# Two of four channel blocks of a depthwise convolution as diagonal fp32 matmuls, in a one-core decoder layer

## The chip, the cores and the metric

One Trainium2 chip, one of its cores, one launch. The metric is the device time of one execution in microseconds (us). Changes of under 0.5% are not told from no change here. Engines are named as the profile names them: PE (TensorE's matmuls), PEld (its weight loads), DVE (VectorE), ACT (ScalarE), POOL (GpSimd) and SP (SyncE, which issues most DMAs).

## The reference, cut to what matters

One layer: a wide input projection, sliding window attention beside a gated causal convolution, an output projection with a layer norm, a product-key mixture of 16384 experts (PEER), and a gated embedding with a second layer norm. The change touches the convolution alone, which has 512 channels and 31 taps per channel:

```python
def conv_group(a, gate, conv_w, conv_b, ln_g, ln_b):
    h = a * jax.nn.sigmoid(gate)
    h = lax.conv_general_dilated(
        h, conv_w[:, None, :].astype(h.dtype), window_strides=(1,),
        padding=((CONV_WIDTH_K - 1, 0),),
        dimension_numbers=('NWC', 'WIO', 'NWC'),
        feature_group_count=CONV_WIDTH) + conv_b
    h = layer_norm(h, ln_g, ln_b)
    return jax.nn.silu(h)
...
        attn = sliding_window_attention(q, k, v, sinks[i])
        conv = conv_group(ca, cg, conv_w[i], conv_b[i], conv_ln_g[i], conv_ln_b[i])
        mixed = jnp.concatenate([attn, conv], axis=-1) @ w_out[i]
        x = layer_norm(DEEPNORM_ALPHA * x + mixed, ln1_g[i], ln1_b[i])
        r = DEEPNORM_ALPHA * x + peer(x, peer_query[i], peer_keys[i], peer_u[i], peer_v[i])
```

The sizes are 1024 tokens and a model width of 1024, in float32.

## The kernel before, in words

The 1024 tokens are 8 tiles of 128. Group A is the first 3 tiles (384 tokens), whose experts are gathered row by row; group B is the other 5 (640 tokens, "dense"), whose experts are computed as full matrix products. Exact products are made of three fp32r matmuls each: an operand is split into a high and a low part (ACT casts the high part `wh` or `acth`, DVE subtracts for the low part `wl` or `actl`), and `mm3` multiplies high by high, high by low and low by high. Attention scores, the values and the sums of the convolution's layer norm are plain fp32 matmuls.

The front of the kernel is made of streams, generators that each yield after a piece of work: `s_x` transposes x, `s_conv` makes the gated input `hc` of the convolution for one block of 128 channels (channels on partitions, 30 tokens of halo and then the group's tokens), `s_taps` applies the 31 taps, `s_qkv` and `s_att` are the attention, `s_cln` is the convolution's layer norm, `s_wout` the output projection and `s_ln1` the first layer norm. Suffix 0 or 1 of a stream is group A or B. The table `ORDER` interleaves the streams by hand in program order. From that program order the framework's scheduler, at build time, fixes the order in which each engine works through its own instructions, and at run time every engine takes them strictly in that order. So an instruction that waits holds up all that stands behind it on its engine.

Before, `s_taps(1)` does for each of four blocks one `tensor_scalar` (line 353, with the bias) and 30 `scalar_tensor_tensor` (line 355) on DVE, each over 128 channels by 640 tokens, accumulating into `cv`. It yields four times a block, 16 times in all, and `ORDER` spreads these 16 steps among the attention of group A and B (`a0`, `a1`), the taps of A and `w0`, the output projection of A. Attention takes a tile of tokens and one of two head groups at a time: PE scores into two PSUM tiles `pt` (line 394), DVE scales and masks them (398) and finds the maxima (404), ACT takes the exponentials (410) and divides (415), PE transposes the probabilities (426), ACT copies them (427), PE multiplies them with the values (430). The PSUM ring `pt` has two buffers, so the scores of one head group and the transposes of another take turns on it.

After the front come the query and top-k stage of A, and then two long stages (`s_early` with the u table and `s_dense` with the v table), in which PE multiplies nearly without a pause while the gathered rows of A run on POOL and DVE.

Of the kernel before, what the change touches and what calls it, by code (L numbers as in the profile page):

```python
# [8 lines left out]
F32 = mybir.dt.float32  # L9
# [4 lines left out]
AF = mybir.ActivationFunctionType  # L14
OP = mybir.AluOpType
# [4 lines left out]
P = 128  # L20
# [6 lines left out]
TAPS = 31  # L27
# [11 lines left out]
SB = 16  # L39
UB = 7  # L40
ROWLAG = 3
LAG = 2
AHEAD = 3
SPILL = 80
# [25 lines left out]
def n_split(n):  # L70
    k = -(-n // 512)
    while n % k or (n // k) % 2:
        k += 1
    return [(i * (n // k), n // k) for i in range(k)]
# [22 lines left out]
def layer(tc, io):  # L97
    nc = tc.nc
# [43 lines left out]
    def ph():  # L142
        return PP.tile([P, 512], F32, name="ph", bufs=4)
# [18 lines left out]
    ident = C.tile([P, P], F32, name="ident")  # L162
# [20 lines left out]
    def page(shape, dt, name):  # L183
        return PG.tile(shape, dt, name=name, tag="page", bufs=PAGES)
# [32 lines left out]
    chan = W_.tile([P, 3, 4], F32, name="chan")  # L217
    cw = W_.tile([P, 4, TAPS], F32, name="cw")
# [126 lines left out]
    def s_taps(gi):  # L345

        n = len(groups[gi]) * P
        cv[gi] = W_.tile([P, 4, n], F32, name="cv", tag=f"cv{gi}")
        for bl in range(4):
            hc, o = cin[gi, bl], cv[gi][:, bl, :]  # L350
            for t in range(TAPS):
                if t == 0:
                    nc.vector.tensor_scalar(o, hc[:, :n], cw[:, bl, 0:1], chan[:, 0, bl:bl + 1], op0=OP.mult, op1=OP.add)
                else:
                    nc.vector.scalar_tensor_tensor(o, hc[:, t:t + n], cw[:, bl, t:t + 1], o, op0=OP.mult, op1=OP.add)
                if t % 8 == 6:
                    yield

    def s_att(gi):

        later = []
        for j, i in enumerate(groups[gi]):
# [73 lines left out]
            for g in range(2):  # L436
                later.append((values, g, scores(g)))
                if len(later) > LAG:
                    f, *a = later.pop(0)
# [318 lines left out]
    def s_gather():  # L758

        for i in GA:  # L760
# [6 lines left out]
            def fetch(table, s):  # L767
                t = G.tile([P, D], F32, name="row", bufs=UB)
                nc.gpsimd.indirect_dma_start(out=t, out_offset=None, in_=table,  # L769
                                             in_offset=bass.IndirectOffsetOnAxis(ap=ids[i][:, s:s + 1], axis=0))  # L770
                return t
# [24 lines left out]
            for f, table, n in order:  # L796
                late.append((f, *divmod(n, SB), fetch(table, n)))
                if len(late) > ROWLAG:
                    g, *a = late.pop(0)
# [19 lines left out]
    def const():  # L819
        constants()  # L820
        yield

    streams = dict(x0=s_x(0), x1=s_x(1), k=const(), c0=s_conv(0), c1=s_conv(1), t0=s_taps(0), t1=s_taps(1), q0=s_qkv(0), q1=s_qkv(1),
                   a0=s_att(0), a1=s_att(1), l0=chain(s_attput(0), s_cln(0)), l1=chain(s_attput(1), s_cln(1)),
                   w0=s_wout(0), w1=s_wout(1), n0=s_ln1(0), n1=s_ln1(1), y=s_query(0), h=s_choose(0), u=early, g=s_swap(), r=rows)
# [90 lines left out]
    n = len(outs) * -(-P // SET)  # L916
# [106 lines left out]
```

## Time and profile before

| | |
|---|---|
| median of 3 runs | 2925.62 us (2921.28 to 2936.11) |
| the profiled execution's own time | 2930.05 us |
| its span in the profile | 2928.2 us |
| mean granted TensorE clock | 0.975 of full speed |
| busy: PE, DVE, ACT, POOL | 95%, 83%, 41%, 37% of the span |
| taps of group B on DVE | 116.5 to about 312 us of the span |

The profile is one execution. A busy time is the time in which at least one instruction of the engine was running, and a granted clock of 1.00 is 2.4 GHz, one of 0.50 is 1.2 GHz. A window's clock in between is a mean over stretches at either level. Idle time of an engine matters only where another one waits for it, so the views used are the windows around the convolution, the chain of work that ended last, and the timeline of single engines.

### The profile page before, as it was taken

To read this page: it belongs to the slowest core of one execution; us is meant where nothing else is said; L and a number is where in the kernel's file an instruction comes from. 1 tells how busy PE (TensorE), PEld (TensorE's weight loads), DVE (VectorE), ACT (ScalarE), POOL (GpSimd) and SP (SyncE) were. 2 spreads that over 40 slices of the span, in tenths; PEclk is the share of its full clock that TensorE was granted. 3 is DMA by queue.
4 is the path that set the end of the run, shared out by engine and by line. 5 is a ranking of instruction groups with operands and counts; after the bars stand their busy time and mean duration, and the time that the engine had idled before them with its cause. 6 is when DMAs were issued, how large, how long until landed. Compare 5 with 4: busy or idle time off the path is not lost.

```text
span 2928.2 us, 47594 instructions
## 1 busy us (share of the span) xinstructions
PE 2794.5 (95%) x17615; PEld 2513.3 (86%) x17615; DVE 2437.2 (83%) x5461; ACT 1193.6 (41%) x2464; POOL 1078.1 (37%) x851
## 2 busy tenths in 40 slices
PE   8996899999999999999999999799899999999888
PEld 8974589999999999999999999687788787777688
DVE  7999768979989799999856666898899888778866
ACT  4454634433334788888622222222222222222143
POOL 0103010267600333443435555555454445444320
PEclk9996899999999999999999999999999999999999
DMA  5211343599913699999999999999999999989631
GB/s 158 76 51 40 99 127 103 183 369 321 349 60 113 239 352 344 334 346 338 364 352 328 338 337 343 364 357 358 352 356 360 358 371 348 323 309 316 215 125 53
DMA packets 324569, 778.11 MB, mean 266 GB/s; under 512 B 29137, under 2 KB 144337, under 8 KB 321776
## 3 DMA queue, kind: packets, MB, share of 16 engines
q0 software_dynamic: 110592, 402.70, 38.0%
q1 hardware_dynamic: 213744, 372.37, 36.5%
q8 instruction: 138, 2.26, 0.3%
q14 instruction: 95, 0.78, 0.1%
HBM read 683.75 MB, written 91.23 MB: 265 GB/s over the span
## 4 chain that ended last, share of the span: by engine, by line
PE 79%; DVE 11%; DMA 5%; issue 3%; ACT 2%; SPq 0%; POOL 0%; DVEq 0%; ACTq 0%; POOLq 0%
PE ph L158 15%; PE ph L159 14%; PE ph L160 14%; PE sum L159 6%; PE sum L158 5%; PE sum L160 5%; PE pv L750 4%; PE pt L659 3%; PE part L158 2%; PE part L159 2%; PE part L160 2%; DMA ge<-e_dr 2%; DVE ag L785 2%; DVE row L777 1%; DVE vl L150 1%
## 5 line engine op out<-in xcount | busy, mean ns | idle before, releaser
L769 POOL DMA_INDIRECT row<-in_peer_u_dram,ids x384 | 511.5, 1332 | 707.9 <-DVE ag L785 418.7
L769 POOL DMA_INDIRECT row<-in_peer_v_dram,ids x384 | 499.5, 1301 | 647.0 <-DVE row L777 480.0
L158 PE MATMUL ph<-acth,uu 128*128 128x320 f32 x2048 | 657.4, 321 | 0.1
L159 PE MATMUL ph<-actl,uu 128*128 128x320 f32 x2048 | 641.6, 313 | 0.0
L160 PE MATMUL ph<-acth,uu 128*128 128x320 f32 x2048 | 639.9, 313 | 0.0
L785 DVE SCALAR_TENSOR_TENSOR ag<-row,hb,ag 128x1024 f32<-128x1024 f32 x384 | 492.4, 1282 | 2.2 <-DMA row<-in_peer_v_dram,ids 1.3
L777 DVE SCALAR_TENSOR_TENSOR row<-row,x 128x1024 f32<-128x1024 f32 x384 | 467.9, 1222 | 5.5 <-DMA row<-in_peer_u_dram,ids 5.2
L158 PEld LDWEIGHTS ph<-acth,uu 128*128 128x128 f32 x2048 | 386.6, 189 | 1.4 <-ACT sg L558 0.4
L159 PEld LDWEIGHTS ph<-actl,uu 128*128 128x128 f32 x2048 | 386.9, 189 | 0.7
L160 PEld LDWEIGHTS ph<-acth,uu 128*128 128x128 f32 x2048 | 385.5, 189 | 0.4
L159 PE MATMUL sum<-vl,ah 128*128 128x512 f32 x896 | 353.7, 395 | 5.0 <-DVE vl L150 4.8
L158 PE MATMUL sum<-vh,ah 128*128 128x512 f32 x896 | 344.2, 397 | 4.2 <-ACT ah L154 2.8
L154 ACT CAST ah<-ge 128x640 fp32r<-128x640 f32 x128 | 93.3, 729 | 570.7 <-DVE ge L878 417.4
L160 PE MATMUL sum<-vh,al 128*128 128x512 f32 x896 | 267.4, 390 | 0.0
L661 ACT CAST uu<-pt 128x512 fp32r<-128x512 f32 x256 | 150.5, 590 | 190.8 <-PE pt L659 181.0
L745 ACT ACTIVATE o<-oo,rest 128x128 bf16<-128x128 bf16 x640 | 205.8, 399 | 21.4 <-DVE oo L740 16.6
L158 PEld LDWEIGHTS sum<-vh,ah 128*128 128x128 f32 x896 | 171.0, 191 | 45.4 <-ACT ah L154 5.4
L159 PEld LDWEIGHTS sum<-vl,ah 128*128 128x128 f32 x896 | 171.3, 191 | 43.2 <-DVE vl L150 7.1
L158 PE MATMUL part<-vh,ah 128*128 128x512 f32 x384 | 154.7, 403 | 47.2 <-ACT ah L154 30.1
L160 PEld LDWEIGHTS sum<-vh,al 128*128 128x128 f32 x896 | 168.5, 188 | 34.9
L150 DVE TENSOR_TENSOR vl<-raw,vh 128x1024 fp32r<-128x1024 f32 x128 | 154.7, 1220 | 40.8 <-ACT vh L154 40.4
L150 DVE TENSOR_TENSOR uu<-pt,uu 128x512 fp32r<-128x512 f32 x116 | 79.8, 689 | 127.7 <-ACT uu L661 118.9
(298 smaller groups left out, 5768.3 us busy)
## 6 DMA issues: line engine op xcount, KB each, us to landing
raw<-in_peer_v_dram SPq DMA_DIRECT2D x128, 512.0 KB
raw<-in_peer_u_dram SPq DMA_DIRECT2D x89, 512.0 KB
e_dr<-ge SPq DMA_DIRECT2D x128, 320.0 KB
g_dr<-stage SPq DMA_DIRECT2D x20, 2048.0 KB
ge<-e_dr SPq DMA_DIRECT2D x128, 320.0 KB
gt<-g_dr SPq DMA_DIRECT2D x21, 1920.0 KB
uraw<-in_peer_u_dram SPq DMA_DIRECT2D x39, 512.0 KB
wraw<-in_peer_query_dram SPq DMA_DIRECT2D x32, 512.0 KB
```

Source lines behind the costliest of these rows:

```text
L150: return eng.tensor_tensor(o, a, b, op=OP.subtract)
L154: nc.scalar.copy(hi, src)
L158: nc.tensor.matmul(ps, lh, rh, start=first, stop=False)
L159: nc.tensor.matmul(ps, lh, rl, start=False, stop=False)
L160: nc.tensor.matmul(ps, ll, rh, start=False, stop=last)
L659: nc.tensor.matmul(ps[:, k * P:(k + 1) * P], raws[c][:, (4 * h + k) * P:(4 * h + k + 1) * P], ident, is_transpose=True, start=k == 0, stop ...
L661: nc.scalar.copy(uu[:, 0], turned)
L745: nc.scalar.mul(o2[:, 2, e], oo[:, 1, e], rest[:, t + e:t + e + 1])
L750: nc.tensor.matmul(ps[:, e * P:(e + 1) * P], o2[:, m, e], oo[:, 0, e], start=m == 0, stop=m == 2)
L769: nc.gpsimd.indirect_dma_start(out=t, out_offset=None, in_=table, in_offset=bass.IndirectOffsetOnAxis(ap=ids[i][:, s:s + 1], axis=0))
L777: behind(nc.vector.scalar_tensor_tensor(u, u, 1.0, x1, op0=OP.mult, op1=OP.mult, accum_out=hb[:, e:e + 1]), marks, TIE)
L785: behind(nc.vector.scalar_tensor_tensor(ag, v, blocks[b][:, e:e + 1], ag, op0=OP.mult, op1=OP.add), marks, TIE)
```

## The change

For blocks 2 and 3 of group B the taps move from DVE to PE. For each tap a 128 by 128 matrix `diag` holds the tap's 128 channel weights on its diagonal, and the convolution is a sum over taps of `diag` times `hc` shifted by the tap, accumulated in two PSUM tiles `ph` of 320 tokens each. DVE builds the diagonal matrices, eight at a time, and ACT moves the sums out of PSUM and adds the bias. A block is now one step of the stream, and six empty steps at the end keep the count of `ORDER` at 16.

```diff
+PE_TAPS = [(1, 2), (1, 3)]
...
         for bl in range(4):
             hc, o = cin[gi, bl], cv[gi][:, bl, :]
+            if (gi, bl) in PE_TAPS:
+
+                pss = [ph()[:, :tn] for _, tn in n_split(n)]
+                for c0 in range(0, TAPS, 8):
+                    m = min(8, TAPS - c0)
+                    diag = page([P, 8, P], F32, "diag")
+                    nc.vector.tensor_tensor(diag[:, :m], ident[:, None, :].to_broadcast([P, m, P]),
+                                            cw[:, bl, c0:c0 + m, None].to_broadcast([P, m, P]), op=OP.mult)
+                    for t in range(c0, c0 + m):
+                        for ps, (t0, tn) in zip(pss, n_split(n)):
+                            nc.tensor.matmul(ps, diag[:, t - c0], hc[:, t + t0:t + t0 + tn], start=t == 0, stop=t == TAPS - 1)
+                for ps, (t0, tn) in zip(pss, n_split(n)):
+                    nc.scalar.activation(o[:, t0:t0 + tn], ps, AF.Identity, bias=chan[:, 0, bl:bl + 1])
+                yield
+                continue
             for t in range(TAPS):
...
+        for _ in range(3 * sum(g == gi for g, _ in PE_TAPS)):
+            yield
```

How the change moves instructions is seen in three places. First, PE before, where the scores of group B's first tile (`pt<-kT,qT`, line 394) stand: layer norm sums of A, then the scores, then the output projection of A (`ph<-wh,actah`).

```order
L430 MATMUL pv<-pT,vlast 64x256
L381 MATMUL pt<-ident,acc_99 128x128 x2
L469 MATMUL pv<-sq,ones 128x384 x3
L394 MATMUL pt<-kT,qT 128x128 x8
L158 MATMUL ph<-wh,actah 128x512
L159 MATMUL ph<-wl,actah 128x512
```

The same place on PE now (line numbers are 18 higher here, and 1 higher in `mm3`): behind the same scores stand all 62 tap matmuls of block 2 in one piece, and then the matmuls that make `hc` of block 3.

```order
L448 MATMUL pv<-pT,vlast 64x256
L399 MATMUL pt<-ident,acc_99 128x128 x2
L487 MATMUL pv<-sq,ones 128x384 x3
L412 MATMUL pt<-kT,qT 128x128 x8
L362 MATMUL ph<-hc,diag 128x320 x62
L159 MATMUL ph<-acth,wh 128x320
L160 MATMUL ph<-actl,wh 128x320
```

Those 48 `hc` matmuls of block 3 (`ph<-acth,wh` and its two partners) stood ahead of the scores before. Now they stand between the two pieces, and the output projection comes after the second piece:

```order
L159 MATMUL ph<-acth,wh 128x320
L160 MATMUL ph<-actl,wh 128x320
L161 MATMUL ph<-acth,wl 128x320
L362 MATMUL ph<-hc,diag 128x320 x62
L159 MATMUL ph<-wh,actah 128x512
L160 MATMUL ph<-wl,actah 128x512
L161 MATMUL ph<-wh,actal 128x512
```

So PE takes the 124 tap matmuls as two unbroken pieces, with nothing of the attention between them; the scores of the second head group come 12 matmuls of the output projection behind the second piece.

Second, DVE before, about 20 us after those first scores: between two operations of the attention (`sc`, `st`) there stand one or two taps (line 355) each time.

```order
L476 TENSOR_TENSOR cv<-cv,rstd 128x384 x4
L405 TENSOR_TENSOR st<-st,sink 128x4
L355 SCALAR_TENSOR_TENSOR cv<-hc,cw,cv 128x640
L404 TENSOR_REDUCE st<-sc 128x4
L355 SCALAR_TENSOR_TENSOR cv<-hc,cw,cv 128x640 x2
L406 TENSOR_TENSOR st<-sink,st 128x4
L355 SCALAR_TENSOR_TENSOR cv<-hc,cw,cv 128x640
```

The same place on DVE now: the diagonal matrices of block 3 are built, `hc` of block 3 is made, two low parts of weights follow, and then the second scores are taken up without a tap between.

```order
L494 TENSOR_TENSOR cv<-cv,rstd 128x384 x4
L358 TENSOR_TENSOR diag<-ident,cw 128x1024 x3
L358 TENSOR_TENSOR diag<-ident,cw 128x896
L340 TENSOR_TENSOR hc<-ph,sg 128x320
L151 TENSOR_TENSOR wl<-wraw,wh 128x1024
L340 TENSOR_TENSOR hc<-ph,sg 128x320
L151 TENSOR_TENSOR wl<-wraw,wh 128x1024
L416 SCALAR_TENSOR_TENSOR sc<-pt,mask 128x2x256 x2
L422 TENSOR_REDUCE st<-sc 128x4
```

The taps of blocks 2 and 3 have left DVE's queue, and the attention's operations stand next to one another.

## Rows read from the trace of the kernel before

**Rows 1.** The page, parts 1 and 4: busy us, share, instructions; the chain by engine.

```profile
PE 2794.5 (95%) x17615; PEld 2513.3 (86%) x17615; DVE 2437.2 (83%) x5461; ACT 1193.6 (41%) x2464; POOL 1078.1 (37%) x851
PE 79%; DVE 11%; DMA 5%; issue 3%; ACT 2%; SPq 0%; POOL 0%; DVEq 0%; ACTq 0%; POOLq 0%
```

**Rows 2.** Windows of the front: busy us by engine, granted clock (PEclk), DMA.

```profile
core 0: us, PE busy (x) PEld busy (x) DVE busy (x) ACT busy (x) POOL busy (x), PEclk, DMA share, GB/s
200.00:360.00 160.00, 123.81 (x579) 83.36 (x577) 134.51 (x220) 90.53 (x225) 23.50 (x28) 0.78 0.20 66
217.00:255.00 38.00, 23.77 (x116) 17.81 (x115) 38.00 (x51) 19.30 (x42) 19.72 (x22) 0.80 0.22 70
255.00:271.00 16.00, 15.21 (x54) 9.30 (x54) 12.85 (x20) 4.02 (x9) 3.78 (x6) 0.51 0.00 0
271.00:280.00 9.00, 1.94 (x18) 1.39 (x18) 8.25 (x15) 5.80 (x21) 0.00 (x0) 0.67 0.00 1
280.00:296.00 16.00, 14.58 (x55) 9.05 (x55) 15.21 (x27) 9.67 (x27) 0.00 (x0) 0.54 0.12 34
296.00:322.00 26.00, 24.71 (x130) 17.71 (x129) 21.48 (x40) 15.95 (x45) 0.00 (x0) 1.00 0.51 156
322.00:349.00 27.00, 16.74 (x82) 11.57 (x82) 18.86 (x38) 17.90 (x47) 0.00 (x0) 0.62 0.27 103
360.00:400.00 40.00, 39.76 (x224) 37.14 (x223) 31.71 (x113) 26.99 (x49) 6.57 (x8) 1.00 0.41 122
```

**Rows 3.** Instructions that write or read cv: ns shortest/median/longest, first and last start us.

```profile
L355 DVE SCALAR_TENSOR_TENSOR cv<-hc,cw,cv x240: 602/800/1631, 30.9 to 311.2; 128x384 f32<-128x384 f32 x60, 128x640 f32<-128x640 f32 x60
L462 PE MATMUL pv<-cv,ones x24: 432/433/590, 204.0 to 379.4; 128*128 128x320 f32 x16, 128*128 128x384 f32 x8
L353 DVE TENSOR_SCALAR cv<-hc,cw,chan x8: 468/542/610, 29.3 to 219.6; 128x384 f32<-128x384 f32 x4, 128x640 f32<-128x640 f32 x4
```

**Rows 4.** Groups by line and shape, 0 to 900 us: busy us, mean ns, idle before.

```profile
L355 DVE SCALAR_TENSOR_TENSOR cv<-hc,cw,cv 128x640 f32<-128x640 f32 x120 | 106.0, 910 | 0.0
L150 DVE TENSOR_TENSOR wl<-wraw,wh 128x1024 fp32r<-128x1024 f32 x76 | 94.2, 1240 | 50.7 <-ACT wh L154 25.5 <-PE pv L159 20.4 <-PE ph L159 2.1
L333 ACT ACTIVATE sg<-ph 128x320 f32<-128x320 f32 x8 | 3.5, 433 | 3.8 <-PE ph L160 3.8
L158 PEld LDWEIGHTS ph<-acth,wh 128*128 128x128 f32 x384 | 72.2, 188 | 1.0 <-ACT sg L333 0.4 <-issue 0.4
```

**Rows 5.** Timeline of PE: start us, us, instruction, count, idle before it and its releaser.

```profile
194.10 0.31 PE L159 MATMUL ph<-actl,wh 128*128 128x320 f32 x1
...
199.09 0.31 PE L160 MATMUL ph<-acth,wl 128*128 128x320 f32 x1
...
210.27 1.03 PE L426 MATMUL pt<-ident,sc 128*128 128x128 f32 x8
...
217.00 1.26 PE L394 MATMUL pt<-kT,qT 64*128 64x128 f32 x16
...
221.19 1.71 PE L394 MATMUL pt<-kT,qT 64*128 64x128 f32 x16
231.52 0.79 PE L158 MATMUL ph<-wh,actah 128*128 128x512 f32 x1 [8.62 <-ACT wh L154]
...
297.18 0.40 PE L158 MATMUL ph<-wh,actah 128*128 128x512 f32 x1
...
299.29 0.39 PE L158 MATMUL ph<-wh,actah 128*128 128x512 f32 x1
...
340.25 3.09 PE L394 MATMUL pt<-kT,qT 64*128 64x128 f32 x16 [1.02 <-DVE actal L150]
...
377.53 2.32 PE L462 MATMUL pv<-cv,ones 128*128 128x320 f32 x8
```

**Rows 6.** Timeline of ACT just before the first scores of group B.

```profile
211.23 0.59 ACT L427 COPY pT<-pt 128x512 f32<-128x512 f32 x1 [3.98 <-PE pt L426]
```

**Rows 7.** The chain of work that ended last, 254 to 297 us: start us, us, what.

```profile
255.38 1.13 PE pt L426 x4
...
258.29 1.04 PE pv L430 x2
259.33 2.00 PE pt L394 x8
261.33 1.90 PE pv L430 x6
...
273.61 0.80 DVE cv L355
...
275.01 0.79 DVE cv L355
...
276.54 1.59 DVE cv L355 x2
```

**Rows 8.** What PE waited for, 400 to 1700 us and 1700 to 2750 us, longest first.

```profile
PE pt L659 <- ACT uu L674: 3.4, 3, 1.6
...
PE part L158 <- ACT ah L154: 30.1, 8, 15.2
PE part L158 <- DVE acc L899: 11.9, 10, 2.0
```

## The prediction

> **What bounds the kernel now.** I read the page first. Over the whole span PE is busy 95% and DVE 83%, and PE holds 79% of the chain that ended last [rows 1]. By that alone, work moved from DVE to PE goes the wrong way; but the taps lie in one short stretch, and the stretch decides. So I read the windows next. From 200 to 360 us DVE is busy 134.51 of 160 us, PE 123.81, and the TensorE clock was granted at 0.78 on average [rows 2]. From 217 to 255 us DVE never stops (38.00 of 38.00), while PE is busy for 23.77 us. Here DVE is the limit, and the taps of blocks 2 and 3 are in its queue. From 360 us on PE is again busy 39.76 of 40 us at full clock [rows 2], and its longest wait up to 1700 us sums to 3.4 us [rows 8]. So what the front gains or loses is handed on whole. The chain says which of the taps are on the path between 255 and 296 us: 0.80, 0.79 and 1.59 us of them [rows 7]. The rest of the path there is PE at an average clock of 0.51 to 0.54 [rows 2].
>
> **What DVE is relieved of.** 60 `scalar_tensor_tensor` of 640 tokens leave, at 106.0/120 = 0.88 us each [rows 4], 53 us, and two `tensor_scalar` at about 0.6 us [rows 3]: 54 us. Eight builds of diagonal matrices come. The trace has none; the nearest row is the subtraction of 1024 fp32 elements at 1.24 us [rows 4], so about 9.5 us (one of four is shorter). If broadcast operands cost double, 20 us, and not under half of it, 5 us. Net, DVE loses some 44 us of 134.51.
>
> **What PE gets.** Plain fp32 matmuls of 320 columns are in the trace: 4 of them show as 8 records, which take 2.32 us with the last one's whole 0.432 us [rows 3, 5]. So records follow one another every (2.32 - 0.43)/7 = 0.27 us, and one matmul takes 0.54 us at full clock. A block is 31 taps by 2 halves: 62 x 0.54 = 33.4 us, both blocks 66.8 us. For comparison, an fp32r matmul of the same width follows the last every (199.09 - 194.10)/34 = 0.147 us [rows 5]. The one thing that could make a tap dearer is its own weight load; those last 0.188 us [rows 4], yet fp32r matmuls with new weights each come every 0.147 us, so loads are hidden there. I take 0.54 us; the upper bound, loads not hidden at all, adds 248 x 0.188 = 47 us. Below 0.54 us I see nothing, since the row has the same type and width.
>
> ACT gets four moves out of PSUM at 0.433 us [rows 4], 1.7 us. They wait for the pieces, and a cast of `wh` and the exponentials of the second scores are queued behind the second pair; but those exponentials wait for PE anyway, and the weights of the next 36 matmuls of the output projection are cast before.
>
> **Where it lands, step by step.** In the new order PE meets the first piece right behind the first scores of group B, which before started at 217.00 us [rows 5]. They come some 3 us sooner: ACT idled 3.98 us just ahead for transposes that stood behind output projection matmuls [rows 5, 6], and these now stand later. So the piece starts at 217 - 3 + 1.1 = 215 us (211 to 219). Its `diag` tiles are ready about then. It ends at 248.5. The 48 matmuls that make `hc` of block 3, moved here, take 48 x 0.147 = 7 us, to 255.6; DVE's copy adds about 0.6 us; the second piece ends at 289.6 us.
>
> DVE meanwhile waits at the diagonals of block 3 for page buffers that the first piece holds, and behind them stand `hc` of block 3 and two low parts of weights. The first three follow as taps finish, and PE has the 7 us of `hc` matmuls to do; so this is hidden, and at worst, all four built late, it costs some 5 us.
>
> Next PE has 84 matmuls of the output projection, at (299.29 - 297.18)/9 = 0.234 us [rows 5], 19.7 us, two more sets of scores at 1.2 us (16 records in 1.26) and six transposes at 0.13 us (8 in 1.03 [rows 5]): 22.9 us. It then reaches the first transposes of group B's probabilities at 312.5 us. Before, they stood at 255.38 us [rows 7]. The change is 57 us late there: two pieces and the moved matmuls (74 us) against about 17 us of DVE-bound waiting that is gone.
>
> **What comes back.** Between 255 and 296 us the taps on the chain, 0.80 + 0.79 + 1.59 = 3.2 us, go [rows 7]. The clock is the other source. Before, PE arrived at 255 us after a stretch in which it was busy 23.77 of 38 us, and ran at 0.51 to 271 us; in 296 to 322 us, where it was busy 24.71 of 26 us, the clock was 1.00 [rows 2]. Now it arrives after 97 us of nearly unbroken matmuls. PE was busy 15.21 us from 255 to 271 us and 14.58 us from 280 to 296 us, both nearly all at the lower level of 1.2 GHz [rows 2], so 7.5 and 7 us could come back. I take 7 us: the first stretch follows straight on dense work, while the second comes after 271 to 280 us, in which PE was busy for 1.94 of 9 us [rows 2]. From 296 us on there is nothing to win from taps, since the last one starts at 311.2 us [rows 3] and is not on the chain. Sum: 57 - 3 - 7 = +47 us.
>
> On this execution's own 2930.05 us that is 2977; it lies 4.4 us over the median of the runs shown, so against the median of 2925.62 I say 2972 us.
>
> **The rest of the kernel.** In the long stages nothing is moved by hand, but the scheduler orders some products of the v table otherwise, and some loads of SP. PE waits there 30.1 us for `ah` and 11.9 us for `acc` [rows 8]; I give this stage 8 us either way and nothing in the sum.
>
> **The rivals.** (A) The clock stays up and attention runs dense: all PE pieces between 255 and 349 us at full clock would give back 7 us more from 280 to 296 and up to 8 us from 322 to 349 us (PE busy 16.74 us at 0.62 [rows 2]), so about +31 us, 2957. The floor is PE without one wait behind the second piece: it has 144 output matmuls (34 us), and eight rounds of scores (1.2 us), transposes (1.0) and values (half of 1.04 + 1.90, which ran at the lower clock [rows 7]), with some 0.2 us for the transposes of queries and keys, 3.9 us each: 65 us up to the last scores, at 354 to 355 us. They stood at 340.25 us before [rows 5]: +14 us, 2940. Against it: PE also waited for ACT and DVE where no tap was left, busy for 16.74 of 27 us [rows 2]. The Trainium skill (Perfetto Trace Analysis, Matmul Optimizations) says that the matmul engine scales power with its use, so that matmuls should come back to back in batches; by that rule this rival is the likelier one, and the trace agrees in kind (1.00 in the dense stretch, 0.51 after the waits).
>
> (B) Faster: the pieces fit into PE's free time, and only DVE's relief counts. PE leaves 36 us of the 160 free and lost time to the clock besides; DVE was the limit, and 44 us less on it gives 2926 - 44 = 2882 at best. It decides if PE's real free time from 200 to 360 us is over 67 us and the attention can run meanwhile. PEld is busy only 83.36 of 160 us, which would leave 77 us [rows 2]. Against it stands the order: both pieces are unbroken, and DVE and ACT get no scores from PE for 74 us. The Trainium skill (Perfetto Trace Analysis, Identifying the Most-Contended Engine) holds the weight loads' busy share, not the matmuls', to be the measure of TensorE's headroom; that is the rule under which this rival would win.
>
> (C) No change: the front is +14 us late or a little less and the long stages swallow part, 2926 to 2940. Against it: PE has almost no slack from 360 to 1700 us [rows 8].
>
> (D) Much slower: the weight loads are not hidden (+47, so 3019), or a piece runs at half clock (+33 each).
>
> **How the numbers follow.** Chances: the forecast (+33 to +66) 0.62, A above the bound 0.20, B 0.03, C 0.06, D 0.09. A measurement of this kernel tells 0.5%, 14.6 us, from no change. Faster 0.03, same 0.07, slower 0.90. The range goes from the floor with something given back by the reordered stage, 2943, to the forecast with a late start, no help from the clock and the 8 us, 2992.
>
> **What would show it.** Right: 248 records on the tap line 0.27 us apart in two runs of 33 us; the first transposes of group B's probabilities near 312 us; the stage after the front shifted by about 47 us; windows between 215 and 290 us with PE full, clock 1.00, and DVE and ACT mostly idle. Wrong: a tap matmul longer or shorter than 0.54 us, a first piece that starts well after 219 us for want of `diag`, a remainder of the attention that needs under 65 or over 110 us, or a v stage that takes some 20 us more or less.

## The result, and the profile after

The changed kernel takes 2971.68 us (median of 4 runs, 2970.06 to 2981.26) and the kernel before, run beside it, 2930.86 us (4 runs, 2921.28 to 2937.76). The ratio is 1.0148, with a 95% interval of 1.0108 to 1.0189: slower, by 1.5%. The prediction was 2972 us.

The page of the kernel after, parts 1 and 4 (before: [rows 1]):

```profile
PE 2850.9 (96%) x17863; PEld 2551.2 (86%) x17863; DVE 2397.4 (81%) x5407; ACT 1194.0 (40%) x2468; POOL 1064.1 (36%) x851
PE 83%; DVE 9%; DMA 4%; issue 2%; ACT 2%; SPq 0%; DVEq 0%; ACTq 0%
```

DVE has lost 39.8 us of busy time and PE has won 56.4. The windows of the front, kernel after (before: [rows 2]):

```profile
core 0: us, PE busy (x) PEld busy (x) DVE busy (x) ACT busy (x) POOL busy (x), PEclk, DMA share, GB/s
215.00:250.00 35.00, 35.00 (x139) 25.28 (x138) 17.12 (x23) 12.16 (x26) 15.00 (x28) 1.00 0.08 24
250.00:290.00 40.00, 40.00 (x166) 29.68 (x165) 2.12 (x3) 2.10 (x3) 0.00 (x0) 1.00 0.07 23
290.00:312.00 22.00, 22.00 (x122) 17.30 (x121) 11.00 (x18) 10.40 (x24) 0.00 (x0) 1.00 0.37 114
312.00:340.00 28.00, 23.97 (x121) 15.68 (x121) 12.51 (x29) 18.12 (x51) 0.00 (x0) 0.76 0.10 29
340.00:400.00 60.00, 50.59 (x256) 34.46 (x255) 36.63 (x73) 40.66 (x104) 0.00 (x0) 0.83 0.28 93
400.00:440.00 40.00, 39.76 (x228) 36.96 (x226) 31.59 (x106) 25.48 (x47) 4.62 (x5) 1.00 0.41 122
```

From 215 to 312 us PE is busy without a gap at full clock, while DVE works for 30 of those 97 us and ACT for 25. The timeline of PE, after (before: [rows 5, 7]), shows what fills the stretch:

```profile
212.84 1.26 PE L412 MATMUL pt<-kT,qT 64*128 64x128 f32 x16
214.04 33.69 PE L362 MATMUL ph<-hc,diag 128*128 128x320 f32 x124
...
254.61 33.57 PE L362 MATMUL ph<-hc,diag 128*128 128x320 f32 x124
...
310.01 0.60 PE L444 MATMUL pt<-ident,sc 128*128 128x128 f32 x4
```

Two unbroken pieces, and behind them the first transposes of group B's probabilities at 310.01 us in place of 255.38: 54.6 us late. The instructions on the tile `diag` and who waited, after:

```profile
L362 PE MATMUL ph<-hc,diag x248: 430/432/537, 214.0 to 287.8; 128*128 128x320 f32 x124
L358 DVE TENSOR_TENSOR diag<-ident,cw x8: 1086/1221/1627, 209.6 to 247.8; 128x1024 f32<-128x1024 f32 x6, 128x896 f32<-128x896 f32 x2
...
  ACT cv L364: 42.6, 2
  DVE diag L358: 13.5, 3
```

The records take 0.432 us each and start between 214.0 and 287.8 us; a diagonal tile costs DVE 1.22 us. ACT waits 42.6 us for the sums of the pieces and DVE 13.5 us for the buffers that they hold. Last, the start of the query stage. Its first work on PE is a transpose of keys (`pt<-ident,kr`); the expectations below call it the first query matmul of tokens A. Before and after:

```profile
L552 PE MATMUL pt<-ident,kr x32: 270/272/476, 361.0 to 798.0; 128*128 128x128 f32 x32
```

```profile
L570 PE MATMUL pt<-ident,kr x32: 270/272/329, 402.5 to 838.9; 128*128 128x128 f32 x32
```

It starts 41.5 us later, and the span ends 2969.6 - 2928.2 = 41.4 us later. All that the change costs, it costs ahead of this row, and the stages behind hand it on. So this row, called the start below, measures the front of every kernel that follows.

### The profile page after: what moved, and what is told of

It is laid out like the page before. It is cut to its first block, busy times and chain, and to the rows that moved or that the text cites. A ratio compares the mean times of both kernels' runs of the same rounds, so it can differ in the third digit from the quotient of the medians.

```text
span 2969.6 us, 48069 instructions
## 1 busy us (share of the span) xinstructions
PE 2850.9 (96%) x17863; PEld 2551.2 (86%) x17863; DVE 2397.4 (81%) x5407; ACT 1194.0 (40%) x2468; POOL 1064.1 (36%) x851
## 4 chain that ended last, share of the span: by engine, by line
PE 83%; DVE 9%; DMA 4%; issue 2%; ACT 2%; SPq 0%; DVEq 0%; ACTq 0%
PE ph L159 15%; PE ph L160 15%; PE ph L161 15%; PE sum L160 6%; PE sum L159 6%; PE sum L161 5%; PE pv L768 4%; PE pt L677 4%; PE ph L362 2%; PE part L159 2%; PE part L160 2%; PE part L161 2%; DMA ge<-e_dr 2%; DVE ag L803 2%; DVE row L795 1%
## 5 line engine op out<-in xcount | busy, mean ns | idle before, releaser
L161 PE MATMUL sum<-vh,al 128*128 128x512 f32 x896 | 277.7, 389 | 1.0 <-DVE al L151 1.0
L763 ACT ACTIVATE o<-oo,rest 128x128 bf16<-128x128 bf16 x640 | 205.3, 397 | 21.5 <-DVE oo L758 18.6
L159 PE MATMUL part<-vh,ah 128*128 128x512 f32 x384 | 154.6, 403 | 46.4 <-ACT ah L155 26.6
```

The lines of the kernel that those rows point to most:

```text
L159: nc.tensor.matmul(ps, lh, rh, start=first, stop=False)
L161: nc.tensor.matmul(ps, ll, rh, start=False, stop=last)
L763: nc.scalar.mul(o2[:, 2, e], oo[:, 1, e], rest[:, t + e:t + e + 1])
```

## The experiments

### Taking the tap matmuls away, or cutting them up

Two kernels ask whether the time is DVE's or PE's. One keeps the change's program order but gives only 2 of the 31 taps of each moved block; the other is the kernel before with 30 of 31 taps of blocks 2 and 3 left out.

```diff
-                for c0 in range(0, TAPS, 8):
-                    m = min(8, TAPS - c0)
+                for c0 in range(0, 2, 8):
+                    m = min(8, 2 - c0)
...
-                            nc.tensor.matmul(ps, diag[:, t - c0], hc[:, t + t0:t + t0 + tn], start=t == 0, stop=t == TAPS - 1)
+                            nc.tensor.matmul(ps, diag[:, t - c0], hc[:, t + t0:t + t0 + tn], start=t == 0, stop=t == 1)
```

> Only the first 2 of the 31 taps of blocks 2 and 3 are done, on PE, with one diagonal tile a block; the other 29 are left out. Theory 1 (all of PE's tap time lies on the path, and DVE's relief gives back about 26 us): each piece shrinks from 33.4 to 2.2 us, so 2971.7 - 62.5 = 2909 us. Theory 1 with a part of the give-back owed to the clock that the long pieces kept up (1.00 until 324 us in the changed kernel): without them the attention starts at the lower clock as before, 7 to 11 us come off the give-back, 2916 to 2920 us. Rival 1 (the relief of DVE is worth nothing, the pieces are partly hidden and cost 41 us in all): about 2930 us, as before.

Measured: 2913.11 us, ratio 0.9940 (0.9919 to 0.9960). The start:

```profile
L570 PE MATMUL pt<-ident,kr x32: 270/272/328, 341.1 to 778.0; 128*128 128x128 f32 x32
```

Against the change at 402.5 us that is 61.4 us earlier for 116 matmuls fewer, which take 116 x 0.54 = 62.6 us. PE's time for taps is exposed nearly whole. The windows from the first transposes of group B's probabilities to the start tell the two theories apart; before, the change, and the change with 2 taps a block:

```profile
255.38:361.00 105.62, 84.10 (x393) 56.01 (x393) 81.69 (x147) 61.54 (x162) 3.46 (x6) 0.73 0.21 70
310.01:402.50 92.49, 78.81 (x401) 53.48 (x399) 51.57 (x107) 61.87 (x161) 0.00 (x0) 0.82 0.23 74
248.50:341.10 92.60, 78.70 (x401) 53.37 (x399) 51.36 (x105) 61.61 (x160) 0.00 (x0) 0.82 0.22 74
```

Behind pieces of 2.2 us this stretch is as long as behind pieces of 33.6 us, at the same clock, so what it gives back against before is not owed to the long pieces. The profiled execution took 2917.34 us, some 8 us over theory 1's 2909, and 6.3 of these lie where no tap is: from the first `sum` matmul to the end it took 1094.6 us, the change 1088.3.

```diff
-                else:
+                elif gi == 0 or bl < 2:
                     nc.vector.scalar_tensor_tensor(o, hc[:, t:t + n], cw[:, bl, t:t + 1], o, op0=OP.mult, op1=OP.add)
```

> The kernel before, with 30 of 31 taps of blocks 2 and 3 left out altogether, neither on DVE nor on PE. It measures what the relief of DVE is worth by itself. Theory 1: 26 us less than before, 2905 us (2895 to 2912). Rival 1 (relief worth nothing): 2925 to 2930 us. Rival 3 (DVE is the only limit there, each us of taps is a us of time): 53 us less, 2878 us.

Measured: 2911.58 us, ratio 0.9941 (0.9924 to 0.9958), start at 342.5 us: 18.5 us earlier than before. That is what DVE's relief by two blocks is worth in about the order of the kernel before. In that of the change it comes to more: the kernel with 2 taps a block starts 19.9 us earlier than before and still has 4.3 us of tap matmuls.

Two kernels with all the work give PE the taps in shorter pieces, one half of the tokens after the other and a pause after 16 taps, so that attention stands between; the diagonals are built twice. The first has both blocks on PE, the second only block 2.

```diff
-                pss = [ph()[:, :tn] for _, tn in n_split(n)]
-                for c0 in range(0, TAPS, 8):
...
+                for t0, tn in n_split(n):
+                    ps = ph()[:, :tn]
+                    for c0 in range(0, TAPS, 8):
...
+                        if c0 % 16 == 8 and c0 < 24:
+                            yield
...
+                    yield
```

> All the work is done. One half of the tokens at a time, cut up: a yield after 16 taps and one after the half, four steps a block in the places of the DVE taps, so PE takes the taps in ten pieces of 4 to 17 us between attention and output projection; the diagonals are built twice (8 more builds on DVE, 10 us). Theory 1 (PE's time is what counts): the pieces can at most fill the waits that PE has in the changed kernel between 312 and 400 us, 88 - 24.0 - 50.6 = 13 us, so 2958 us, 2952 to 2965. Rival 2 (the loss comes from two unbroken pieces that hold up the attention): cut up, the taps fit into PE's waits and DVE's relief counts, 2930 us or less.

Measured: 2962.95 us, within the range of theory 1, ratio 1.0117 (1.0099 to 1.0136), start at 392.7 us. Cutting up is worth 9.8 us of the front; the other 31.7 us stay.

> All the work is done. Block 2 alone goes to PE, cut up as in the run with quarters (one half of the tokens at a time, a yield after 16 taps and after the half); block 3 stays on DVE. Theory 1: 33.4 us of PE, half of the relief back (13 us), and up to 13 us of it in PE's waits: 2930 + 33 - 13 - (0 to 13) = 2937 to 2950 us. Rival 2: it fits into the 38 - 23.8 + 9 - 1.9 = 21 us that PE waited between 217 and 280 us before, and is faster than before, 2915 to 2925 us.

Measured: 2912.90 us, ratio 0.9949 (0.9932 to 0.9966): faster than the kernel before and than the change, under the ranges of both theories, and not by the front, as its start shows:

```profile
L569 PE MATMUL pt<-ident,kr x32: 270/272/473, 361.8 to 798.4; 128*128 128x128 f32 x32
```

The front is 0.8 us later than before, but the span is 20.1 us shorter. Something behind the front had changed, and that needed runs of its own.

### One block, and every tap twice

> All the work; only block 2 on PE, in the one piece that the change gives it (124 records, 33.4 us), block 3's taps stay on DVE, so DVE builds 4 diagonal tiles. Read by the start of the first query matmul of tokens A (361.0 before, 402.5 with both blocks on PE, 361.8 with block 2 alone in pieces), since the v stage behind it is written in an order of its own here (1067 to 1095 us). Theory (a tap's PE time counts in full, the relief of DVE is what is paid back): with half of the 25 us of relief 361 + 33.4 - 12 = 382; if one block's relief is already worth most of the 18.5 us that two gave, 361 + 33.4 - 18 = 376. Rival (one block fits beside the dense attention's waits however it is written, as the version in pieces suggests): 362. So a start at 376 to 382 says that the cutting up was worth 14 to 20 us, one at 362 that it was worth nothing.

```diff
-PE_TAPS = [(1, 2), (1, 3)]
+PE_TAPS = [(1, 2)]
```

Measured: 2948.05 us, ratio 1.0071 (1.0053 to 1.0090). The start:

```profile
L570 PE MATMUL pt<-ident,kr x32: 270/272/473, 368.4 to 804.6; 128*128 128x128 f32 x32
```

Neither value expected came: 7.4 us later than before, and 6.6 us later than the same block in pieces. The second block of the change adds 402.5 - 368.4 = 34.1 us, its matmuls' 33.4 us in full.

> The kernel before with 30 of the 31 taps of block 2 of the dense group left out: the relief of DVE by one block (26 us) without any tap matmul. Both blocks left out moved the first query matmul of tokens A from 361.0 to 342.5. If relief goes by DVE's time: 352 (-9). If DVE held up the front by no more than one block's taps: 343 (-18). If the last block alone is waited for: 361 (0). Its written order of the v stage is the same as that of the version with block 2 on PE in one piece, so from the first sum to the end the two should agree within 5 us.

```diff
-                else:
+                elif (gi, bl) != (1, 2):
                     nc.vector.scalar_tensor_tensor(o, hc[:, t:t + n], cw[:, bl, t:t + 1], o, op0=OP.mult, op1=OP.add)
```

Measured: 2919.39 us, ratio 0.9968 (0.9955 to 0.9981), start at 343.7 us: 17.3 us earlier than before, where two blocks gave 18.5. The first block's relief is worth nearly everything and the second's 1.2 us. From the first `sum` matmul to the end it takes 1099.3 us, and the version with block 2 uncut 1097.8, within 5 us as expected. So one block uncut should have cost 33.4 - 17.3 = 16.1 us, but costs 7.4. In the windows of the version with block 2 uncut the granted clock reads 1.00 from 215 to 290 us, where the kernel before ran at 0.51 to 0.80 from 217 to 296 us [rows 2]:

```profile
215.00:250.00 35.00, 35.00 (x141) 25.36 (x140) 11.46 (x19) 12.16 (x26) 12.50 (x28) 1.00 0.09 29
250.00:290.00 40.00, 38.02 (x224) 29.51 (x222) 31.82 (x50) 18.50 (x41) 0.00 (x0) 1.00 0.21 68
```

The clock is not the whole of the missing 8.7 us. From 204 us to the first transposes of group B's probabilities, first with block 2's taps left out, then with block 2 uncut, and what PE waited for in the first of the two:

```profile
204.00:254.90 50.90, 37.33 (x171) 25.99 (x170) 48.86 (x66) 28.05 (x59) 18.78 (x21) 0.83 0.19 63
204.00:276.20 72.20, 71.63 (x345) 53.20 (x344) 41.84 (x62) 28.27 (x60) 12.50 (x28) 1.00 0.14 45
PE ph L158 <- ACT wh L154: 10.2, 2, 8.4
PE ph L158 <- ACT actah L154: 2.8, 1, 2.8
```

With the taps left out PE has 13.6 us without work here, 13.0 of them for casts on ACT; with the piece it has 0.6. So the piece fills waits of the output projection that DVE's relief had left. Behind, from the first transposes to the start, the piece gives nothing back: 92.2 us, against 88.8 with the taps left out, both at a clock of 0.85. The clock ahead (1.00 for 0.83) has a share too, but the orders of the two kernels differ as well, and no run here separates the shares.

> The change with every tap matmul given twice into the same sum (the two blocks come out with twice their convolution): 248 further records of PE. Theory (PE's time is the bound of the front, nothing hides a tap): 66.8 us later, first query matmul of tokens A at 402.5 + 67 = 469, span near 3037, median 3039, ratio to before 1.037. Rival (waits and a lower clock around the pieces give part of it back, as the front gave back 14 us of the 54.6 in the change): 2.5 to 3 per cent over before, 3005 to 3020.

```diff
-    nc.tensor.matmul(ps, diag[:, t - c0], hc[:, t + t0:t + t0 + tn], start=t == 0, stop=t == TAPS - 1)
+    nc.tensor.matmul(ps, diag[:, t - c0], hc[:, t + t0:t + t0 + tn], start=t == 0, stop=False)
+    nc.tensor.matmul(ps, diag[:, t - c0], hc[:, t + t0:t + t0 + tn], start=False, stop=t == TAPS - 1)
```

Measured: 3037.99 us, ratio 1.0377 (1.0358 to 1.0396). The start:

```profile
L571 PE MATMUL pt<-ident,kr x32: 270/272/328, 469.2 to 905.6; 128*128 128x128 f32 x32
```

66.7 us later than the change, for 124 matmuls that take 124 x 0.54 = 67 us. The rival, that part is given back, falls.

Four versions give PE a block's taps in one piece, in nearly the order of the change (some 35 of 1759 other records ahead of the start stand elsewhere): with 4.3, 33.4, 66.8 and 134 us of tap matmuls they start at 341.1, 368.4, 402.5 and 469.2 us. Less the matmuls these are 336.8, 335.0, 335.7 and 335.2. So in this order each tap on PE costs its time, and what is set against it is nearly fixed, 24 to 26 us off the 361.0 of before, with one block moved as with two.

### Where the 20 us behind the front come from

The v stage and the end, from the first `sum` matmul on, have the same instructions in all kernels, but the scheduler writes them in different orders. In the windows of this stretch, 1087.3 us long before and 1067.3 us in the version with block 2 in pieces, PE runs 4879 matmul records both times. The window of before:

```profile
1840.90:2928.20 1087.30, 1024.30 (x4879) 853.23 (x4877) 897.89 (x1189) 269.92 (x346) 472.21 (x328) 0.98 0.85 304
```

And of the version with block 2 in pieces:

```profile
1840.80:2908.10 1067.30, 1014.50 (x4879) 847.79 (x4877) 898.08 (x1189) 271.32 (x346) 458.39 (x328) 0.98 0.86 309
```

PE has 52.8 us without work in place of 63.0, and is busy 9.8 us less for the same records. To tell an effect of the taps from one of the order, the pauses of the taps on DVE were moved, which alters the order alone; in two of the three kernels the last taps then also come too late for the layer norm, as said there.

> All the work of the kernel before, no tap on PE: only the places where block 2's taps of the dense group hand over to the other steps move by two taps (after taps 5, 13, 21 and 29 of 31, in place of 7, 15, 23 and 31). In the written order of PE this swaps four transposes in the front; from the first sum of the v stage on PE's order is then, instruction for instruction, that of the version with block 2 alone on PE in pieces, which ran 17.5 us under the kernel before with an unchanged front. Theory (those 17 to 20 us are the written order of the v stage and not the taps): first query matmul of tokens A at 361 us as before, from the first sum to the end 1067 us in place of 1087, profiled span near 2908, median 2912, ratio 0.994. Rival (they come from the taps on PE, which left DVE or the clock better off later): span 2928, ratio 1.000.

```diff
-                if t % 8 == 6:
+                if t % 8 == (4 if (gi, bl) == (1, 2) else 6):
```

Measured: 2931.59 us, ratio 1.0011 (0.9999 to 1.0022). The expectation rested on a mistake: PE's written order in this program is that of the kernel before, row for row. So the run decides nothing on the question; with the same order it takes nearly the same time, 1090.0 us from the first `sum` to the end and 1087.3 before.

> All the work of the kernel before, no tap on PE: only block 3's taps of the dense group hand over to the other steps two taps earlier (after taps 5, 13, 21 and 29 of 31). This one does what was meant by the run with block 2's pauses moved, whose written order of PE turned out to be that of the kernel before, row for row: here four transposes change places in the front, and the last 14135 of 17962 rows of PE's written order, 2286 of DVE's, 1247 of ACT's and 488 of SP's are those of the version with block 2 alone on PE in pieces. Theory (that version's 17.5 us are the written order of the v stage): first query matmul of tokens A at 361 us as before, first sum to end 1067 us in place of 1087, span near 2908, median 2912, ratio 0.994. Rival (they come from the taps on PE, or from a lucky phase of two streams of transfers): span 2928 and ratio 1.000.

```diff
-                if t % 8 == 6:
+                if t % 8 == (4 if (gi, bl) == (1, 3) else 6):
```

Here the taps of block 3 behind its last pause are added only when the layer norm has already read the sums, so the output lacks them; all instructions still run. Measured: 2907.74 us, ratio 0.9928 (0.9914 to 0.9941), with no tap on PE. The start is at 356.8 us, 4.2 us earlier. The missing wait is not the reason: before, the layer norm's matmuls of group B start at 349.1 us, and the last tap at 311.2. What is stays open. Of the other 21 us 18 are in the later stretch:

```profile
1833.60:2902.70 1069.10, 1012.22 (x4879) 845.10 (x4877) 897.98 (x1189) 271.60 (x346) 458.70 (x328) 0.99 0.86 309
```

> The change, both blocks on PE in one piece each, with the pauses of the taps left on DVE one tap earlier in both groups: the later part of PE's written order (the last 14135 rows) is then that of the version with block 2 alone on PE in pieces. Theory (the v stage's length goes by its written order): first query matmul of tokens A near 402 as in the change (the front's order moves a little too: 395 to 410), first sum to end 1067 in place of 1088, span near 2949, median 2951, ratio 1.007 to before. Rival (order does nothing): 2970, ratio 1.0145.

```diff
-                if t % 8 == 6:
+                if t % 8 == 5:
```

Here the last tap of group A's block 3 comes behind its layer norm in the same way, and the output lacks it. Measured: 2952.10 us, ratio 1.0081 (1.0068 to 1.0095), start at 404.7 us, and then:

```profile
1881.70:2952.60 1070.90, 1015.12 (x4879) 847.63 (x4877) 898.21 (x1189) 271.26 (x346) 458.73 (x328) 0.98 0.86 308
```

So the change, with this written order of the v stage, is some 20 us shorter, and the stretch takes 1067 to 1071 us whatever stands in the front. With the order of before it takes 1087 to 1090, and in the change 1088.3:

```profile
1881.30:2969.60 1088.30, 1023.30 (x4879) 850.47 (x4877) 899.14 (x1189) 269.24 (x346) 474.28 (x328) 0.98 0.85 304
```

The traces bear this out. In the stretch PE's records follow one another in the same sequence in the version with block 2 in pieces, in the last two kernels and in the one with eight taps below: 1067.2, 1069.1, 1070.9 and 1069.4 us. Kernels that share another sequence come out 1.0 us (1087.8 and 1088.8), 1.5 us (1097.8 and 1099.3) and 2.7 us (1087.3 and 1090.0) apart. The widest pair is the change and its version with 2 taps a block, 1088.3 and 1094.6 us, so one execution can differ by some 6 us in one order.

### Fewer taps on PE

> All the work; taps 0 to 15 of block 2 on PE, one half of the tokens and then the other (32 matmuls, 64 records, 17.2 us), taps 16 to 30 added on DVE to what ACT wrote, block 3 on DVE. Theory (PE's taps cost their time, and the first block's worth of DVE's relief is what pays: 17.3 us for 26 us of taps taken from DVE, so about 9 for these 13 us less two diagonal tiles twice; pieces between the dense attention's waits and a full clock give back some 15): first query matmul of tokens A at 361 + 17 - 9 - 10 = 359, between 352 and 366. Rival (each part is counted by PE's time alone): 361 + 17 - 9 = 369. The v stage is written in yet another order, so only the front is read, and the span lies at 2905 to 2940.

```diff
+            on_pe = PE_HALF if (gi, bl) == (1, 2) else 0
+            if on_pe:
+                for t0, tn in n_split(n):
...
-            for t in range(TAPS):
+            for t in range(on_pe, TAPS):
```

Measured: 2927.12 us, ratio 0.9996 (0.9982 to 1.0009), start at 355.7 us: 5.3 us earlier than before. The start is within the range expected. Its v stage is not of the short kind (1089.5 us), and the time is that of before.

> All the work; taps 0 to 7 of block 2 on PE (16 matmuls, 32 records, 8.6 us), the other 23 added on DVE, block 3 on DVE, with one pause between the two halves of the tokens. The last 14135 rows of PE's written order are those of the version with block 2 alone on PE in pieces. Theory (front by PE's time less relief and clock, as sixteen taps gave 5.3 us less than before; the v stage by its written order): first query matmul of tokens A between 354 and 361, first sum to end 1067 to 1071, span 2901 to 2910, median near 2909, ratio 0.993. Rival (the shorter v stage came with the two kernels whose taps end late and with a whole block on PE, and is not to be had with this front): first sum to end 1087 to 1090, span near 2924, ratio 0.9985.

```diff
-PE_HALF = 16
+PE_HALF = 8
...
                     nc.scalar.activation(o[:, t0:t0 + tn], ps, AF.Identity, bias=chan[:, 0, bl:bl + 1])
-                    yield
+                    if t0 == 0:
+                        yield
```

Measured: 2903.41 us (2902.17 to 2904.34), ratio 0.9914 (0.9897 to 0.9931), the fastest version here that does all the work. Both the start and the later stretch are as the theory had them:

```profile
L568 PE MATMUL pt<-ident,kr x32: 270/272/329, 354.6 to 790.0; 128*128 128x128 f32 x32
```

```profile
1832.20:2901.60 1069.40, 1014.70 (x4879) 847.05 (x4877) 897.79 (x1189) 271.12 (x346) 458.83 (x328) 0.99 0.86 309
```

Of its 26.6 us of span, 6.4 are the front's and 17.9 the later stretch's.

The fronts of all versions in a table. The matmul time is 0.54 us for each tap and half of the tokens. Each start is that of one profiled execution.

| version | tap matmuls on PE, us | start, us | against before, us |
|---|---|---|---|
| before, block 2's pauses moved | 0 | 360.8 | -0.2 |
| before, block 3's pauses moved | 0 | 356.8 | -4.2 |
| before, two blocks' taps left out | 0 | 342.5 | -18.5 |
| before, block 2's taps left out | 0 | 343.7 | -17.3 |
| 2 taps of each block on PE, 29 left out | 4.3 | 341.1 | -19.9 |
| 8 taps of block 2 on PE | 8.6 | 354.6 | -6.4 |
| 16 taps of block 2 on PE | 17.2 | 355.7 | -5.3 |
| block 2 on PE, in pieces | 33.4 | 361.8 | +0.8 |
| block 2 on PE, uncut | 33.4 | 368.4 | +7.4 |
| blocks 2 and 3, in pieces | 66.8 | 392.7 | +31.7 |
| blocks 2 and 3, uncut (the change) | 66.8 | 402.5 | +41.5 |
| the change, other taps' pauses moved | 66.8 | 404.7 | +43.7 |
| the change, every tap twice | 134 | 469.2 | +108.2 |

## Why the prediction was right

**The bound.** It was said that what the front gains or loses is handed on whole. The start moved by 41.5 us and the end by 41.4.

**DVE's relief.** The cost of the diagonals was right (8 x 1.22 = 9.8 us, for 9.5). Only part of the 44 us net was on the path: with two blocks' taps gone and nothing in their place the front moves by 18.5 us, with one block's by 17.3. The prediction priced the relief at 17 us of waiting plus 3.2 us of taps on the chain, and 18.5 us lies close to that. But the 17 us were not all bound by DVE: from 204 us to the first transposes PE waits 14.9 us before and still 9.2 with both blocks' taps left out, 8.1 of them for casts on ACT; with 2 taps a block in the order of the change it waits 1.2. So most of that waiting went with the order. Rival B counted all 44 us and came to 2882; its mechanism was wrong, and so was its price, since leaving the taps out altogether gives no better than 2911.58.

**PE's price.** 123 steps in 33.69 - 0.43 us are 0.270 us a record, 0.54 us a matmul, as worked out from 8 records of another matmul. Weight loads add nothing to that, even in a stretch where each pair of matmuls has a new matrix, so rival D's +47 us is out. The Trainium skill (Perfetto Trace Analysis, Identifying the Most-Contended Engine), named beside rival B, judges TensorE's headroom by two measures, the matmul work done against the peak and the weight loads' busy share. By the second alone, which the prediction took, a piece would leave 28% free: from 215 to 250 us PEld is busy 25.28 of 35 us. The runs differ: a second copy of every tap in these pieces cost its 67 us in full.

**Where it lands.** First piece at 215, measured 214.04; second at 256, measured 254.61; transposes at 312.5, measured 310.01. The wait of DVE for page buffers was 13.5 us and hidden, as argued.

**What comes back.** Of the 54.6 us the query stage sees 41.5, so 13.1 came back; 10 were predicted. This is the term that was mis-sized: +47 predicted, +41.5 measured, 2.5 us of it in the landing and 3 in the give-back. The parts of the give-back were off by more, and so was the reason. From the first transposes to the start PE waits 7.8 us less than before (21.5 and 13.7 us) and is busy 5.3 us less (84.10 and 78.81); the prediction had 3 us of taps and 7 of clock. It put the clock down to 97 us of nearly unbroken matmuls ahead. But with 2 taps a block, and so without the long pieces, the stretch takes 92.60 us at the same clock of 0.82, and with both blocks' taps left out and no tap on PE 93.8 us at 0.82. So this part came with DVE's relief. The clock stayed at 1.00 in all windows from 215 to 312 us, so some of rival A was true, but from 312 to 400 us it is 0.76 and 0.83 again, with PE busy 74.56 of 88 us. The floor of rival A was not reached.

**The median.** 2977 us were predicted for an execution that before had taken 2930.05; the profiled execution of the change took 2971.58. The 4.4 us subtracted to meet the median of the runs shown had no ground, as the kernel before had a median of 2930.86 beside the change. So the close agreement of 2972 with 2971.68 is luck: two errors of some 5 us cancel. Two small sums of the prediction do not close either, without bearing on the result: rival A leaves 47 - 7 - 8 = 32 us and not 31, and the lower end of the range, 2943, lies above the floor of 2940 from which something was to be taken.

**The v stage.** Here the 8 us either way were too few as a rule: by its written order the stretch takes 1067 to 1071 us, or 1087 to 1095, or up to 1099 in the orders seen. For the change it happened to be 1.0 us longer, which is luck as well. Had its order come out as in the version with other pauses, the time would have been 2952. Which rows of the order make the short kind short is not settled: the waits are shorter and PE is busy less for the same records (52.8 for 63.0 us and 1014.50 for 1024.30, with block 2 in pieces), but the runs changed the order as a whole.

## What to carry to other kernels

Price a move between engines where it lands: a tap cost DVE 0.88 us, of which 17.3/30 = 0.58 us were exposed in the first block and 1.2/30 = 0.04 us in the second, and PE 1.08 us, which were exposed in full from the second block on. Relief of a busy engine pays only until something else is waited for (here one block of 26 us, worth 17), while the engine that takes over pays for every microsecond beyond its idle time (here some 13 us of waits, which the first block filled). So move a little, in pieces: the Trainium skill (Perfetto Trace Analysis, Optimization Strategy) suggests interleaving regimes that have different limits, and in this case pieces between the attention were worth 9.8 us for two blocks and 6.6 for one. How much of the 6.4 us of the version with eight taps is owed to them stays open, since 4.2 us also came with moved pauses and no tap on PE. And where a scheduler writes the order, compare stage by stage, by one row at each stage's start, before a gain is put down to the edit: two thirds of the best version's gain were the order of a stage that the edit does not touch.

## What the runs showed that was not expected

ACT's move of a tap sum out of PSUM with a bias took 0.527 us for 128x320, where the Sigmoid of the same shape, which is given no bias, takes 0.433 [rows 4]. Whether the function or the bias makes the 0.094 us no run here separates. The instructions of the line, kernel after:

```profile
L364 ACT ACTIVATE cv<-ph,chan x4: 527/527/528, 247.2 to 288.2; 128x320 f32<-128x320 f32 x4
```

A stage of the same 4879 matmul records took 1067 to 1099 us by its written order, which is more than the front's whole gain or loss with one block on PE.
